# Sixteen experts in two forms: sorted by token count on the chip, the six smallest in plain float32 with gate and up side by side in TensorE's columns

## The chip, the cores and the metric

One core of one Trainium2 chip runs the whole kernel in one launch. The metric is the device time of one execution in microseconds (us), median of the runs shown. The two versions are compared on the same inputs.

## The reference, cut to what matters

Two layers run over 512 tokens of width 1024. Each has a part of mixers (attention, gated linear attention, mLSTM), then a mixture of experts, then a gated per-layer embedding. The mixture, on normalised tokens `t`:

```python
gi  = argmax(t @ w_group + b_group)               # one of 4 groups
el  = (t @ w_router + b_router)[group gi]          # its 4 experts
top_v, top_i = top_k(el, 2)
top_w = softmax(top_v) * softmax(group logits)[gi]
for e in range(16):
    a = silu(t @ w_gate[e]) * (t @ w_up[e])        # 1024 -> 512
    y = y + comb[:, e] * (a @ w_down[e])           # 512 -> 1024
```

Each token goes to two of the 16 experts, so an expert has 64 tokens on average. The reference's own routing of its inputs gives, with experts 0 and 1 left out and the other fourteen sorted, 73 72 72 71 71 70 65 62 and then 61 60 58 55 46 45 tokens in the first layer, and 106 98 91 87 65 65 61 56 and then 53 53 48 48 46 44 in the second.

## The kernel before, in words

All tensors are float32. Where precision matters a matmul is made of three: both factors are split into a high and a low part of type float32r (`split` and `hilo`: ScalarE copies the high part, VectorE subtracts it), and `mm3` (L328) multiplies high by high, high by low and low by high.

`moe` (L1294) does one layer's mixture. The token rows are stored to DRAM (`xd`, L1297). Routing: rank comparisons give each token's two experts, a cumulative count on TensorE gives its place in the expert's list, and `rows`, `places` and `to_rows` turn this into lists of row numbers, one column for each expert: `ix` (row to gather) and `iy` (row to scatter to). `parts` and `to_parts` bring two scales for each row the same way, `sw`: the combine weight and the token's inverse norm.

The experts run in the order 0 to 15. For expert `e`:

- `fetch(e)` (L1588) gathers up to `CAP` = 112 rows by an indirect DMA on GpSimd's queue; numbers past the count are out of bounds and move nothing. `scale` multiplies by the norm's gain.
- `x_T` and `x_split` transpose the rows (8 transposes of 128 columns) and split them.
- `gate_up(c, u)`: eight calls, four for gate and four for up. Each splits two of the eight 128-row blocks of the weight matrix and issues 6 matmuls of 512 columns: 48 for gate and up together.
- `silu`, `times`, `a_T` (4 transposes), `a_split`, and `down(k)` for four k: 24 matmuls of 512 columns.
- `store` (L1538) copies the result times its weight to `YE` and scatters the rows into `yd` in DRAM by an indirect DMA (L1548).

The loop (L1598) staggers this: round `e` does the gate and up of expert `e`, the transposes of expert `e`+1, the down matmuls of expert `e`-1 and the store of expert `e`-2.

Weights come by plain DMAs on SyncE's queue (`load`, L259): 1 MB each, two for gate, two for up, two for down, 6 MB for an expert. Sixteen buffers of 1 MB take turns (`E8O`), so a load waits until the sixteenth load before it has been split. The first loads are issued while the mixers still run; the sixteenth goes to ScalarE's queue (`late`). After expert 15 the per-layer embedding follows: `ple_prep` and `ple_rows` multiply the embedding (`PR`), a branch (L1680) handles experts with over 112 tokens, and the rows of `yd` are loaded as `Y` (L1729) and added to `X` (L1755). Everything after that needs `X`.

A scheduler sets the order of instructions on each engine from the program's order and its own costs.

Of the kernel before, what the change touches and what calls it, by code (L numbers as in the profile page):

```python
# [14 lines left out]
I32 = mybir.dt.int32  # L15
# [12 lines left out]
CAP = 112  # L28
# [38 lines left out]
def tile_encoder(ctx: ExitStack, tc: tile.TileContext, A, out):  # L67
# [132 lines left out]
    v.tensor_copy(tok, ti)  # L200
    cs_.__exit__(None, None, None)
# [46 lines left out]
    def load(src, eng=nc.sync):  # L248
# [9 lines left out]
        late = NQ < st["n"] <= E8  # L258
        i = (nc.scalar if late else eng).dma_start(wv, src)  # L259
        if late:  # L260
            order(st["ex"], i)
        elif NP < st["n"] <= E8 + 1:
            order(st["xd"], i)
# [302 lines left out]
    def mixers(l, T_):  # L566
# [652 lines left out]
        def router_weights():  # L1219
# [8 lines left out]
            g.tensor_tensor(wr3, wr3, bc(gc.unsqueeze(2), [128, 8, 20]), OP.mult)  # L1228
            wrs = small("wrs", 320, F32R, bufs=1)
# [64 lines left out]
    def moe(l, X, rsx, lg3):  # L1294
# [75 lines left out]
        def parts():  # L1370

            V = t2("V2")[:, 0:384].bitcast(BF16).rearrange("p (j i c e) -> p j i c e", j=N8, i=3, c=2)
            ra = small("ra", 2 * N8, bufs=1)
            rb_ = small("rb_", 2 * N8, BF16, bufs=1)
            g.tensor_copy(ra[:, 0:N8], w12)
            g.tensor_copy(ra[:, N8:2 * N8].rearrange("p (k t) -> p k t", k=2), bc(rsx.unsqueeze(1), [128, 2, NT]))
            for i in range(3):
                g.tensor_copy(rb_, ra)
                st["parts"] = g.tensor_tensor(V[:, :, i, :, :], bc(oh3.unsqueeze(2), [128, N8, 2, 16]),
                                bc(rb_.rearrange("p (c j) -> p j c", c=2).unsqueeze(3), [128, N8, 2, 16]), OP.mult)  # L1380
                if i < 2:
                    g.tensor_tensor(ra, ra, rb_, OP.subtract)
            return V

        def to_rows(dst, V, O, c):

            ps = mm()[:, 0:16]
            for j in range(N8):
                pe.matmul(ps, O[:, j, :], V[:, j, 0, :], start=(j == 0), stop=False)
                st["pe"] = pe.matmul(ps, O[:, j, :], V[:, j, 1 + c, :], start=False, stop=(j == N8 - 1))  # L1390
            return v.tensor_scalar(dst, ps, 1024.0 * (1 + c), None, OP.add)

        def to_parts(dst, V, O):

            ps = mm()[:, 0:32]
            for j in range(N8):
                for i in range(3):
                    pe.matmul(ps, O[:, j, :], V[:, j, i].rearrange("p c e -> p (c e)"), start=(j == i == 0), stop=(j == N8 - 1 and i == 2))
            act(dst, ps, AF.Copy)
# [5 lines left out]
        ix, iy = small("ix", 16, I32, bufs=1), small("iy", 16, I32, bufs=1)  # L1405
        st["gate"] = to_rows(ix, V1, OH, 0)
# [5 lines left out]
        to_rows(iy, V1, OH, 1)  # L1412
        st["wm"] = warm(W2, st["pe"])
        cmax = small("cmax", 1, bufs=1)
        after(v.tensor_reduce(cmax, pos[:, 64:80], AX.X, OP.max))
        cmi = small("cmi", 17, I32, bufs=1)
        v.tensor_copy(cmi[:, 16:17], cmax)
        after(v.tensor_copy(cmi[:, 0:16], pos[:, 64:80]))
# [24 lines left out]
        sw = small("sw", 32, bufs=1)  # L1443
# [26 lines left out]
        class Expert:  # L1470


            def __init__(self, n, w_, xe, iyc, swc, rsc, m=CAP):
                self.n, self.w, self.xe, self.iyc, self.swc, self.rsc, self.m = n, w_, xe, iyc[0:m], swc[0:m], rsc[0:m], m
# [17 lines left out]
            def gate_up(self, c, u):  # L1492

                if u == 0:
# [15 lines left out]
            def times(self):  # L1510
                v.scalar_tensor_tensor(self.a, self.pu[0:self.m], self.rsc, self.a, OP.mult, OP.mult)
# [15 lines left out]
            def down(self, k):  # L1527

                if k == 0:
                    self.py = [zb(), zb()]  # L1530
# [3 lines left out]
                for half in range(2):  # L1534
                    hs = slice(half * 512, half * 512 + 512)
                    _, self.last = mm3(self.py[half][0:self.m], self.ah[:, k, :], self.al[:, k, :], hi[:, 0, hs], lo[:, 0, hs], k == 0, k == 3)

            def store(self, both=False):  # L1538
# [4 lines left out]
                act(ye[:, 0:512], self.py[0][0:self.m], AF.Copy, scale=self.swc)  # L1543
# [307 lines left out]
```

## Time and profile before

| what | value |
|---|---|
| median of 3 runs (lowest, highest) | 1462.6 us (1461.03, 1466.82) |
| profiled execution: its own time, its span | 1467.49 us, 1465.8 us |
| granted TensorE clock, mean | 0.978 |
| TensorE, VectorE, ScalarE, GpSimd busy | 95%, 82%, 67%, 23% |
| moved by DMA | 304.39 MB, 208 GB/s over the span |

The span runs from the first instruction to the last; the execution's own time is 1.7 us more. The two mixtures lie at about 350 to 669 us and 1075 to 1393 us. A matmul's duration in a row includes the time it takes to run through the array, which the next ones overlap, so the pace of matmuls is read from the distances of their starts.

### The profile page before, as it was taken

What the parts mean: (1) busy time and instruction counts of PE and PEld (TensorE: products, weight loads), DVE (VectorE), ACT (ScalarE), POOL (GpSimd) and SP (SyncE); (2) the same over time, 40 slices, a digit from 0 to 9 for tenths busy, and PEclk for the clock granted to TensorE, in tenths of its full rate; (3) what the DMA queues carried; (4) which work ended last, traced back from release to release, by engine and by line L of the source; (5) the groups of instructions that cost most, each with busy time, mean ns of one, the idle gap of its engine ahead of it and who ended that gap; (6) DMA issues with size and microseconds to landing.
All of it is one profiled execution on the core that took longest, in us unless ns stands there. A gap on an engine that the chain in (4) does not pass through costs nothing. (4 is left out here: it accounts for less than half of the span.)

```text
span 1465.8 us, 23792 instructions
## 1 busy us (share of the span) xinstructions
PE 1386.5 (95%) x8468; PEld 1139.5 (78%) x8468; DVE 1197.9 (82%) x2057; ACT 981.5 (67%) x1747; POOL 338.8 (23%) x356
## 2 busy tenths in 40 slices
PE   6998999998899999998989989999979999999997
PEld 5787878995677777777967878789957777777787
DVE  5779887567799999997667788866679999999875
ACT  5553675645688888886555546655458888888864
POOL 4223000211243333312012230002013434333000
PEclk9999999999899999999979999999989999999999
DMA  6321133648799999937133112326478999999271
GB/s 164 102 65 54 58 85 83 230 139 298 234 380 379 374 375 374 380 109 255 49 122 100 56 32 72 102 80 227 162 277 297 371 371 373 365 360 357 92 245 58
DMA packets 171235, 304.39 MB, mean 208 GB/s; under 512 B 30368, under 2 KB 69316, under 8 KB 171108
## 3 DMA queue, kind: packets, MB, share of 16 engines
q1 hardware_dynamic: 142656, 277.91, 54.7%
q0 software_dynamic: 9024, 18.99, 3.8%
q10 hardware_dynamic: 19428, 5.88, 1.7%
q8 instruction: 69, 1.13, 0.3%
q14 instruction: 58, 0.48, 0.1%
HBM read 285.90 MB, written 23.13 MB: 211 GB/s over the span
## 5 line engine op out<-in xcount | busy, mean ns | idle before, releaser
L293 DVE TENSOR_TENSOR lo<-we,hi 128x1024 fp32r<-128x1024 f32 x380 | 447.3, 1222 | 17.7 <-PE mm L330 5.8
L237 ACT ACTIVATE hi<-we 128x1024 fp32r<-128x1024 f32 x380 | 396.4, 1059 | 78.9 <-PE mm L331 46.1
L329 PE MATMUL mm<-hi,xhl 128*112 128x512 f32 x480 | 193.4, 403 | 0.3 <-POOL gqattn_k_norm_g L611 0.3
L331 PE MATMUL mm<-hi,xhl 128*112 128x512 f32 x480 | 191.3, 399 | 1.3 <-DVE xhl L336 1.3
L1548 POOL DMA_INDIRECT yd<-YE,iy x32 | 143.2, 4475 | 203.0 <-ACT YE L237 81.7
L330 PE MATMUL mm<-lo,xhl 128*112 128x512 f32 x480 | 190.0, 396 | 0.0
L482 PE MATMUL zb<-hi,Th 128*128 128x256 f32 x576 | 169.3, 295 | 0.0
L483 PE MATMUL zb<-lo,Th 128*128 128x256 f32 x576 | 163.1, 283 | 0.0
L484 PE MATMUL zb<-hi,Tl 128*128 128x256 f32 x576 | 162.3, 282 | 0.0
L482 PEld LDWEIGHTS zb<-hi,Th 128*128 128x128 f32 x576 | 109.0, 190 | 8.8 <-issue 8.0
L483 PEld LDWEIGHTS zb<-lo,Th 128*128 128x128 f32 x576 | 109.2, 190 | 2.9 <-issue 1.7
L484 PEld LDWEIGHTS zb<-hi,Tl 128*128 128x128 f32 x576 | 108.9, 189 | 1.5 <-issue 1.3
L331 PEld LDWEIGHTS mm<-hi,xhl 128*112 128x112 f32 x480 | 84.4, 176 | 29.3 <-DVE xhl L336 1.4
L330 PEld LDWEIGHTS mm<-lo,xhl 128*112 128x112 f32 x480 | 84.7, 176 | 26.5
L329 PEld LDWEIGHTS mm<-hi,xhl 128*112 128x112 f32 x480 | 84.7, 176 | 25.6 <-POOL gqattn_k_norm_g L611 0.5
L329 PE MATMUL zb<-hi,ah 128*112 128x512 f32 x256 | 103.4, 404 | 1.0 <-ACT ah L237 1.0
L331 PE MATMUL zb<-hi,al 128*112 128x512 f32 x256 | 101.4, 397 | 0.0
L330 PE MATMUL zb<-lo,ah 128*112 128x512 f32 x256 | 101.1, 395 | 0.0
L293 DVE TENSOR_TENSOR lo<-w,hi 128x1024 fp32r<-128x1024 f32 (+3 forms) x66 | 74.9, 1134 | 24.3 <-PE zb L483 18.0
L237 ACT ACTIVATE hi<-w 128x1024 fp32r<-128x1024 f32 (+3 forms) x66 | 63.0, 955 | 38.3 <-PE zb L484 35.8
L237 ACT ACTIVATE P<-mm,nm 128x512 f32<-128x512 f32 x64 | 44.0, 688 | 39.4 <-DVE nm L1012 39.0
L482 PE MATMUL zb<-hi,mh 128*128 128x256 f32 x224 | 65.0, 290 | 1.4 <-DVE X L1134 1.4
(426 smaller groups left out, 3278.3 us busy)
## 6 DMA issues: line engine op xcount, KB each, us to landing
we<-in_w_expert_up_dram SPq DMA_DIRECT2D x64, 1024.0 KB, 11.7
we<-in_w_expert_down_dram SPq DMA_DIRECT2D x64, 1024.0 KB, 12.8
we<-in_w_expert_gate_dram SPq DMA_DIRECT2D x60, 1024.0 KB, 12.0
w<-in_w_in_dram SPq DMA_DIRECT2D x44, 512.0 KB, 3.8
we<-in_w_ple_gate_dram SPq DMA_DIRECT2D x8, 1024.0 KB, 9.7
Y<-yd SPq DMA_DIRECT2D x16, 512.0 KB, 9.5
X<-xd SPq DMA_DIRECT2D x12, 512.0 KB, 4.0
w<-in_w_out_dram SPq DMA_DIRECT2D x10, 512.0 KB, 4.4
```

Of the source, the lines that this page charges most:

```text
L237: i = s.activation(out_, in_, func, **kw)
L293: i = (g if eng == "g" else v).tensor_tensor(l3, src, h3.bitcast(F32), OP.subtract)
L329: i = pe.matmul(ps, ah, bh, start=start, stop=False)
L330: pe.matmul(ps, ah, bl, start=False, stop=False)
L331: return i, pe.matmul(ps, al, bh, start=False, stop=stop)
L482: pe.matmul(pt[tb], ah[c][:, sl], hi, start=(k == 0 and (by_tb or tb % 2 == 0)), stop=False, skip_group_check=True)
L483: pe.matmul(pt[tb], ah[c][:, sl], lo, start=False, stop=False, skip_group_check=True)
L484: pe.matmul(pt[tb], al[c][:, sl], hi, start=False, stop=(k == nk - 1), skip_group_check=True)
L1548: st["sc"] = g.indirect_dma_start(out=yv[self.n], out_offset=bass.IndirectOffsetOnAxis(ap=self.iyc, axis=0), in_=ye, in_offset=None, bound ...
```

## The change

The experts get 16 slots. Slots 0 and 1 hold experts 0 and 1 always; the other fourteen are ranked by token count, largest first, by comparisons on VectorE (`c2`, `se`, `eq`). `by_slot` permutes the expert numbers (`pi`) and the lists of rows and scales (`ixs`, `iys`, `rps`) into slot order. SyncE reads each slot's expert number from `pi` into a register, and the loads of slots 2 to 15 take their address from it. Slots 0 to 9 run as before; slots 10 to 15 are of class `Small`: 64 rows at most, the factors unsplit in float32, gate's result in PSUM partitions 0 to 63 and up's in 64 to 127, so that gate's weights-by-rows matmul uses one half of the array's columns and up's the other; `down` does the same with its two halves of 512 output columns. The combine weight moves from `store` to the addition of `Y`, where it is a column for each token (`wr`). The branch now runs for a count above 112 in a big slot or above 64 in a small one. All loads go by SyncE's queue.

```diff
-CAP = 112
+CAP, CAPS, NBIG = 112, 64, 10
...
-        late = NQ < st["n"] <= E8
-        i = (nc.scalar if late else eng).dma_start(wv, src)
+        i = eng.dma_start(wv, src)
...
+        sq_ = t2("eq")
+        aux, eq = [sq_[:, c:c + 256].rearrange("p (s e) -> p s e", s=16) for c in (0, 256)]
+        cn = small("cn", 16, bufs=1)
+        after(v.tensor_copy(cn, pos[:, 64:80]))
+        c2, se = small("c2", 16, bufs=1), small("se", 16, bufs=1)
+        v.scalar_tensor_tensor(c2, cn, 16.0, tie, OP.mult, OP.add)
+        v.tensor_tensor(aux, bc(c2.unsqueeze(1), [128, 16, 16]), bc(c2.unsqueeze(2), [128, 16, 16]), OP.is_gt)
+        v.tensor_reduce(se, aux, AX.X, OP.add)
+        v.tensor_tensor(eq, bc(se.unsqueeze(1), [128, 16, 16]), bc(io16.unsqueeze(2), [128, 16, 16]), OP.is_equal)
+
+        def by_slot(dst, src):
+
+            v.tensor_tensor(aux, eq, bc(src.unsqueeze(1), [128, 16, 16]), OP.mult)
+            return v.tensor_reduce(dst, aux, AX.X, OP.add)
...
+        by_slot(pf, io16)
+        v.tensor_copy(pi, pf)
...
+        class Small(Expert):
...
+            def x_split(self, q):
+                if q == 0:
+                    self.x = r3(t8("xhl")[:, 0:512], 8)
+                    v.tensor_tensor(self.x, r3(self.ps, 8), bc(st["gc"].unsqueeze(2), [128, 8, 64]), OP.mult)
+
+            def gate_up(self, k):
+
+                if k == 0:
+                    self.pg = mm()
+                if k % 4 == 0:
+                    self.rw = [load(self.w(nm).rearrange("(k p) n -> p k n", p=128)[:, k:k + 4, :]) for nm in ("w_expert_gate", "w_expert_up")]
+                for c in range(2):
+                    pe.matmul(self.pg[64 * c:64 * c + 64], self.x[:, k, :], self.rw[c][:, k % 4, :], start=(k == 0), stop=(k == KD - 1))
...
+            def down(self, k):
...
+                for h in range(2):
+                    pe.matmul(self.py[h], self.aT[:, k, :], self.rd[k][:, 0, h * 512:h * 512 + 512], start=(k == 0), stop=(k == 3))
...
+            m, ic = (CAP if e < NBIG else CAPS), (ix if e < 2 else ixs)[:, e:e + 1]
+            if e < 2:
+                w_ = lambda nm: A[nm][l, e]
+            else:
+                pv = nc.values_load(pi[0:1, e:e + 1], engines=[mybir.EngineType.SP], min_val=0, max_val=15)
+                w_ = lambda nm: A[nm][l][bass.DynSlice(pv, 1)].rearrange("o k n -> (o k) n")
+            EX.append((Expert if e < NBIG else Small)(e, w_, gather(ic, e, m), iys[:, e:e + 1], rps[:, e:e + 1], m))
...
-        with tc.If(cnt > CAP):
+        with tc.If(cnt > 0):
...
-                    i = (g if (tb, h) in XA else v).tensor_tensor(X[tb][:, hs], X[tb][:, hs], Y[tb][:, k, hs], OP.add)
+                    i = v.scalar_tensor_tensor(X[tb][:, hs], Y[tb][:, k, hs], wr[:, c:c + 1], X[tb][:, hs], OP.mult, OP.add)
```

SyncE's queue, first layer, from the loads of the first experts to the first ones that need the sort. Before:

```order
L259 DMA we<-in_w_expert_down_dram 128x2x1024 x2
L259 DMA we<-in_w_expert_gate_dram 128x4x512 x2
L259 DMA we<-in_w_expert_up_dram 128x4x512 x2
L1297 DMA xd<-X 128x1024 x4
L259 DMA we<-in_w_expert_down_dram 128x2x1024 x2
L1679 TENSOR_LOAD cmi
```

And now (`pi` is the list of expert numbers; the `ISA` rows set registers):

```order
L265 DMA we<-in_w_expert_down_dram 128x2x1024 x3
L1302 DMA xd<-X 128x1024 x4
L265 DMA we<-in_w_expert_down_dram 128x2x1024
L1686 TENSOR_LOAD pi
L1686 ISA x2
...
L265 ISA
L265 DMA we<-in_w_expert_gate_dram 128x4x512
L265 ISA
L265 DMA we<-in_w_expert_gate_dram 128x4x512
```

The four loads of expert 2's gate and up stood ahead of the store of `xd`; those of slot 2 now stand behind it and behind the reading of `pi`.

VectorE, first layer, from the first list of rows to the scaling of the first gathered rows (`lo<-W` is a weight split, `XE` the gathered rows, `xhl` the split of the transposed rows). Before:

```order
L1391 TENSOR_SCALAR ix<-mm 128x16
...
L1442 TENSOR_TENSOR w_4593<-w_4593,ex 128x4
L293 TENSOR_TENSOR lo<-W_4461,hi 128x1024
L1466 TENSOR_TENSOR XE<-XE,gain 112x1024
L293 TENSOR_TENSOR lo<-W_4461,hi 128x1024
L1466 TENSOR_TENSOR XE<-XE,gain 112x1024
L336 TENSOR_TENSOR xhl<-tp,xhl 128x4x112 x2
```

And now:

```order
L1400 TENSOR_SCALAR ix<-mm 128x16
...
L1482 TENSOR_TENSOR w_4625<-w_4625,ex 128x4
L1508 TENSOR_TENSOR XE<-XE,gain 112x1024
L1438 TENSOR_REDUCE pf<-eq 128x16
L297 TENSOR_TENSOR lo<-W_4467,hi 128x1024
L1400 TENSOR_SCALAR iys<-pf 128x16
L340 TENSOR_TENSOR xhl<-tp,xhl 128x4x112 x2
L297 TENSOR_TENSOR lo<-W_4467,hi 128x1024
L1508 TENSOR_TENSOR XE<-XE,gain 112x1024
```

Between the first row and the row of `w` the sort adds 15 instructions, 8 of them of 256 elements. The first expert's `xhl` no longer stands behind the scaling of the second expert's rows.

TensorE at the end of the first layer's mixture as it is now (a row counts a float32 matmul once; `we` is a weight buffer, `aT` the transposed activations):

```order
L1614 MATMUL mm<-we,xhl 64x512 x16
L1640 MATMUL zb<-we,aT 64x512 x4
L1626 MATMUL tp<-ident,a 128x64 x4
L1640 MATMUL zb<-we,aT 64x512 x12
L1655 MATMUL tp<-ident,p 128x128 x8
L1775 TENSOR_LOAD cmi
```

These are the gate and up of slot 15, the down matmuls of slots 14 and 15 and the transposes of the embedding. The 48 and 24 matmuls of the last expert before have become 16 and 8.

## Rows read from the trace of the kernel before

**Rows 1.** Stretches: length, engines' busy time (instructions), clock, DMA share, GB/s
```profile
340.00:380.00 40.00, 28.64 (x179) 18.36 (x178) 27.89 (x69) 21.64 (x41) 9.48 (x15) 0.79 0.70 245
460.00:500.00 40.00, 40.00 (x188) 30.50 (x187) 38.89 (x39) 34.97 (x42) 16.99 (x7) 1.00 1.04 376
620.00:660.00 40.00, 39.48 (x184) 29.96 (x183) 36.82 (x36) 34.81 (x41) 7.09 (x3) 1.00 0.36 131
```

**Rows 2.** Transposes of gathered rows, eight an expert: their line, 440 to 640; timeline
```profile
L1481 PE MATMUL tp<-ident,XE x88: 257/259/260, 453.9 to 633.5; 112*128 112x112 f32 x88
...
632.81 0.93 PE L1481 MATMUL tp<-ident,XE 112*128 112x112 f32 x8
```

**Rows 3.** Weight loads by tile: all from 412.6, then the first, the last, `p`
```profile
L259 SPq DMA_DIRECT2D we<-in_w_expert_gate_dram x21: 367/368/368, 412.7 to 591.3; - x21
...
DMA to landing us min/median/max: 9.0/9.0/9.0
...
DMA to landing us min/median/max: 16.6/16.6/16.6
...
L1553 SPq DMA_DIRECT2D p<-in_p_dram x1: 368/368/368, 614.9 to 614.9; - x1
...
DMA to landing us min/median/max: 13.8/13.8/13.8
```

**Rows 4.** Second layer's last expert but one load, by tile
```profile
L259 SPq DMA_DIRECT2D we<-in_w_expert_down_dram x1: 994/994/994, 1336.0 to 1336.0; - x1
...
DMA to landing us min/median/max: 15.2/15.2/15.2
```

**Rows 5.** Timeline, ends of both mixtures: TensorE, the last scatter, the first load of `Y`
```profile
663.47 0.60 PE L1564 MATMUL tp<-ident,p 128*128 128x128 f32 x4
665.18 0.94 POOL L1548 DMA_INDIRECT yd<-YE,iy  x1 [6.60 <-ACTq L1680]
669.14 0.90 SPq L1729 DMA_DIRECT2D Y<-yd  x2
...
1387.00 0.60 PE L1564 MATMUL tp<-ident,p 128*128 128x128 f32 x4
1392.68 1.68 SPq L1729 DMA_DIRECT2D Y<-yd  x3
```

**Rows 6.** Scatters into `yd` by tile, issued at 622.65 and at 665.18: time to landing
```profile
DMA to landing us min/median/max: 9.7/9.7/9.7
...
DMA to landing us min/median/max: 3.8/3.8/3.8
```

**Rows 7.** Timeline of TensorE: float32 in column halves (L889) and whole (L873)
```profile
63.43 1.08 PE L889 MATMUL mm<-tT,la 128*64 128x256 f32 x8
64.44 0.39 PE L482 MATMUL zb<-hi,Th 128*128 128x256 f32 x1
...
70.48 1.02 PE L873 MATMUL mm<-la,tR 128*128 128x256 f32 x4
71.34 0.38 PE L878 MATMUL mm<-ident,qk 128*128 128x128 f32 x2
```

**Rows 8.** Timeline, routing and first expert: VectorE, SyncE, TensorE
```profile
357.60 0.42 DVE L1359 TENSOR_TENSOR V<-oh,tok 128x256 bf16<-128x256 f32 x1
363.03 0.21 DVE L1439 TENSOR_SCALAR w<-ex 128x4 f32<-128x4 f32 x1 [1.20 <-ACT ex L237]
363.76 1.23 DVE L293 TENSOR_TENSOR lo<-W,hi 128x1024 fp32r<-128x1024 f32 x1
367.83 1.23 DVE L1466 TENSOR_TENSOR XE<-XE,gain 112x1024 f32<-112x1024 f32 x1 [2.85 <-DMA XE<-xd,ix]
...
335.74 0.92 SPq L259 DMA_DIRECT2D we<-in_w_expert_gate_dram  x2
...
375.00 0.63 PE L329 MATMUL mm<-hi,xhl 128*112 128x512 f32 x1
375.42 0.63 PE L330 MATMUL mm<-lo,xhl 128*112 128x512 f32 x1
```

More of the change, by code (lines that the diff above doesn't have):

```diff
@@ L200, in tile_encoder @@
     v.tensor_copy(tok, ti)
+    io16 = const.tile([128, 16], F32, name="io16")
+    v.tensor_copy(io16, ii[:, 0:16])
+    tie = const.tile([128, 16], F32, name="tie")
+    v.tensor_scalar(tie, io16, -1.0, 15.0, OP.mult, OP.add)
+    for n in range(2):
+        v.memset(tie[:, n:n + 1], 65536.0 * (2 - n))
     cs_.__exit__(None, None, None)
@@ L1370, in parts @@
         def parts():
[L1372 to L1376, printed above, removed]
+            V = t2("V2")[:, 0:192].bitcast(BF16).rearrange("p (j i e) -> p j i e", j=N8, i=3)
+            ra = small("ra", NT, bufs=1)
+            rb_ = small("rb_", NT, BF16, bufs=1)
+            g.tensor_copy(ra, rsx)
             for i in range(3):
                 g.tensor_copy(rb_, ra)
-                st["parts"] = g.tensor_tensor(V[:, :, i, :, :], bc(oh3.unsqueeze(2), [128, N8, 2, 16]),
-                                bc(rb_.rearrange("p (c j) -> p j c", c=2).unsqueeze(3), [128, N8, 2, 16]), OP.mult)
+                for k in range(2):
+                    js = slice(k * NT, k * NT + NT)
+                    st["parts"] = g.tensor_tensor(V[:, js, i, :], oh3[:, js], bc(rb_.unsqueeze(2), [128, NT, 16]), OP.mult)
                 if i < 2:
@@ L1404, in moe @@
         OH = places()
-        ix, iy = small("ix", 16, I32, bufs=1), small("iy", 16, I32, bufs=1)
-        st["gate"] = to_rows(ix, V1, OH, 0)
+        ix, iy, ixs, iys = [small(nm, 16, I32, bufs=1) for nm in ("ix", "iy", "ixs", "iys")]
+        psx = to_rows(V1, OH, 0)
+        st["gate"] = number(ix, psx, 0)
         def after(i):
@@ L1535, in down @@
                     hs = slice(half * 512, half * 512 + 512)
[L1536 removed]
+                    mm3(self.py[half], self.ah[:, k, :], self.al[:, k, :], hi[:, 0, hs], lo[:, 0, hs], k == 0, k == 3)
             def store(self, both=False):
@@ L1691, in moe @@
                     ce = nc.values_load(cc[0:1, 0:1], min_val=0, max_val=T)
-                    with tc.If(ce > CAP):
+                    with tc.If(ce > 0):
                         ic, jc = [small(nm, 1, I32, bufs=1) for nm in ("ic", "jc")]
-                        wc, rc_ = [small(nm, 1, bufs=1) for nm in ("wc", "rc_")]
-                        for d_, s_, o_ in ((ic, ix, 0), (jc, iy, 0), (wc, sw, 0), (rc_, sw, 16)):
-                            v.tensor_copy(d_, s_[:, bass.DynSlice(e_ + o_, 1)])
+                        rc_ = small("rc_", 1, bufs=1)
+                        for d_, s_ in ((ic, ix), (jc, iy), (rc_, rp)):
+                            v.tensor_copy(d_, s_[:, bass.DynSlice(e_, 1)])
                         w_ = lambda nm: A[nm][l][bass.DynSlice(e_, 1)].rearrange("o k n -> (o k) n")
-                        ex = Expert(16, w_, gather(ic, 0, 128), jc, wc, rc_, 128)
+                        ex = Expert(16, w_, gather(ic, 0, 128), jc, rc_, 128)
                         scale(ex.xe, 128)
@@ L1702, in moe @@
                             ex.x_split(q)
-                        for c in range(2):
-                            for u in range(4):
-                                turn[0] = s0 + 6 + c
-                                ex.gate_up(c, u)
+                        for u in range(8):
+                            turn[0] = s0 + 6 + u // 4
+                            ex.gate_up(u)
                         ex.silu()
```

114 lines of the change are left out of this document (74 added, 40 removed).

## The prediction

> **What bounds the kernel now.** I read the stretches first, then the weight loads by tile, then the ends of the two mixtures. In the middle of a mixture TensorE is busy 40.00 us of 40, and the DMA engines are full as well, a share of 1.04 at 376 GB/s [rows 1]. Two limits lie close together, and the change moves only one of them, so each needs its own pace.
>
> TensorE's pace: the transposes of eleven experts begin between 453.9 and 633.5. Less the 0.7 us between the first and the last of one expert's eight, that is 178.9 us for ten experts, **17.9 us an expert** [rows 2]. The DMA engines' pace: the gate load issued at 412.7 landed after 9.0 us, the one at 591.3 after 16.6. They are twenty gate loads apart, two an expert, so ten experts. The landings lie at 421.7 and 607.9, **18.6 us an expert** [rows 3]. The engines are slower than TensorE uses the weights up, and the delay grows by 0.7 us an expert. That is why I count them as full and don't expect them to go faster.
>
> Yet the weights don't set the end. The embedding `p`, issued behind the last weights, landed at 614.9 + 13.8 = 628.7. Its 0.5 MB take 1.4 us at 376 GB/s, so the last weights were there at 627.3 [rows 1, 3]. TensorE finished the last down matmul at 663.5 [rows 5]. For 36 us it worked off full buffers, with the DMA share down at 0.36 [rows 1]. In the second layer the last load but one landed at 1336.0 + 15.2 = 1351.2, the last 2.8 us later (1 MB), at 1354.0 [rows 4]; TensorE finished at 1387.0, 33 us later [rows 5]. From TensorE's end to the first load of `Y`, which all that follows needs, it is 5.7 us in both layers [rows 5].
>
> **The small experts on TensorE.** A float32 matmul leaves two records in the trace. Whole-array ones of 256 columns start 0.215 us apart (four from 70.48, the next matmul at 71.34). In column halves eight such records take 1.01 us (63.43 to 64.44) [rows 7]. Taking turns they would need 8 x 0.215 = 1.72; in pairs 4 x 0.215 = 0.86. So the halves run together, and 0.15 is left over, which I count once for each change between halves and whole. For 512 columns a step is 0.43. Gate and up take 8 blocks x 2 steps, down 4 x 2: 24 x 0.43 = 10.3 us. Twelve transposes take at most 0.12 each (0.93 / 8, [rows 2]), 1.4; they have 64 columns in place of 112, so half of that at the low end. Four changes of form add 0.6. Together 11 to 12.3, and I take **12**. If the 0.15 were not fixed but a share of the work (1.01 / 0.86), the 10.3 would be 12.1 and the expert 14.1; this is the high end.
>
> "Mode switching requires drain", says the Trainium skill (TensorEngine Tiling, Key Properties). It speaks against a form that alternates halves with whole-array transposes, and the 0.15 agrees with a small drain. By the rule alone, without a figure, the sum could not be made.
>
> Six experts save 6 x (17.9 - 12) = 35.4 us of TensorE a layer. The weights limit what of this is seen: the small expert needs 12 us and its weights 18.6. After the last load only the last two blocks of down are left, 4 steps, 1.7 us. First layer: TensorE's limit is 663.5 - 35.4 = 628.1, the weights' limit 627.3 + 1.7 = 629.0. Second layer: 1387.0 - 35.4 = 1351.6 and 1354.0 + 1.7 = 1355.7. The weights win in both, and TensorE ends 34.5 and 31.3 us earlier.
>
> **What follows the last matmul.** `YE`, the branch and the scatter remain, 5.7 us. But the scatter used to meet idle DMA engines and landed in 3.8 us; under load one took 9.7 [rows 6]. Now it comes right behind the weights, among `p`, the embedding's weights and `X`, 3.5 MB or 9.3 us of transfers. So 0 to 6 us are given back a layer; being issued some 4 us into that queue, it gets the middle, 3. Gains: 31.5 and 28.3, **59.8 us**. TensorE's embedding matmuls, which run beside the loads of `Y`, move with it; the embedding's weights land about 3 us after the experts', still ahead of `Y`.
>
> **The sort.** It puts 15 instructions on VectorE between the first list of rows and the first scaling: 8 of 256 elements at 0.42 and 7 small ones at about 0.18, 4.6 us. There VectorE sat idle 1.20 and 2.85 us, and the weight split of 1.23 goes behind [rows 8]. This covers 5.3, and the scaling waits for the gathered rows in any case: cost 0. Without that cover it would be 4.6 a layer. The first expert's low parts no longer wait behind the second expert's gather, which may give up to 2 us back; I take none, because the weight split has moved behind. Gather lists of slot 2 and scatter lists are needed later.
>
> **The loads that now wait for the sort.** Expert 2's gate and up were issued at 335.7 and just after, before the store of `xd` [rows 8]. Now four loads, and the one that went by ScalarE's queue, wait for `pi`, at about 365. Four take 4 x 2.8 = 11.2 us. The DMA engines were 30% idle between 340 and 380, 12 us [rows 1], and the slot starts only two experts after the first, near 410. So they fit: cost 0, but tightly, and 11.2 us a layer if they don't, as every later load queues behind them. Behind SyncE's wait stand only loads of later slots. Its register settings are small beside the 3.0 us between loads (17.9 / 6); an issue takes 0.46.
>
> **Edits at nothing.** Splits that go, on ScalarE and VectorE, were paced by TensorE. The combine weight is one more operand in an addition that is made anyway. The small experts' gather moves no fewer bytes: numbers out of bounds never moved. The second layer's router gain is now loaded late, behind slot 15's `x_split`, ahead of the last silu on ScalarE; it has one expert's 18.6 us to land.
>
> **The sum.** 1467.5 - 59.8 = 1407.7 for the profiled execution, which was 4.9 above the median of the runs: **1403**. Differences under 0.5% can't be told from none here.
>
> **Rivals.**
> - *The early loads are not caught up* (or a small expert takes 14.1). For it: 12 us of idle for 11.2 us of loads, and the idle lies partly before `pi` is there. Against: the buffers are full by 380 either way, and the engines have slack until about 400. Price 11.2 a layer: 1425. For 14.1: 6 x 2.1 = 13 less, the first layer then ends near 641, about the same price.
> - *The clock stays low, slower.* Small experts leave TensorE idle a third of the time. Between 340 and 380, busy 28.64 of 40, the granted clock was 0.79 on average, and the first expert's matmuls ran at the lower of the two levels, 1.2 GHz, 0.42 us apart [rows 1, 8]. At 1.2 GHz a step is 0.86, the expert 24 x 0.86 + 2 = 22.6. From 17.9 on it is a loss: 6 x 4.7 = 28 a layer, 1519. Against: at 22.6 TensorE would be behind the weights and would not pause, and without pauses it was granted 1.00 [rows 1]. So it decides only if the clock stays low under steady work. Pauses in matmul work bring the half clock, says the Trainium skill (TensorE: Matmul & The Clock Gate, HAM oscillation); the trace agrees in its 0.79. By that rule alone, held through all small experts, the time would be that of this rival.
> - *The halves take turns at 512 columns, slower.* 48 x 0.43 + 2 = 22.6, the same 1519. Against: rows 7, unless twice the columns change it.
> - *It doesn't do what it says:* were a small slot over 64 tokens, the branch would run. By the reference's routing the largest small slot has 61 and 53, no big one over 106. Then there is no gain or a large loss.
>
> **Chances.** Forecast 0.75, with 1388 to 1418 as its own range: 3 us a layer either way from the scatter, 2 a layer from the start, some from the weights' pace. The first rival 0.15, at 1418 to 1432. The two slower ones 0.05 and 0.03, no gain 0.02. The range goes from 1386 to 1428, which leaves out the slow cases and the worst of the first rival. Faster by over 0.5% holds the forecast and the first rival, with a little off for what I have not seen: 0.90; within 0.5%: 0.02; slower: 0.08.
>
> **What would show it.** Right: in the last third of each mixture TensorE is busy about two thirds, with DMA still near 375 GB/s until the last weights; small records in pairs of starts, steps of 0.43; the first load of `Y` near 638 in the first layer, the second layer's about 60 earlier than now; VectorE's first scaling still waits for the gather. Wrong: a DMA gap before slot 2's loads with weights landing 11 us later (first rival); steps of 0.86 or single starts (the slower ones); instructions of the branch's body.

## The result, and the profile after

| | before | after |
|---|---|---|
| median of 4 runs each, one chip | 1461.82 us (1460.81 to 1466.82) | 1417.28 us (1415.28 to 1418.67) |
| profiled execution: own time, span | 1467.49, 1465.8 us | 1418.6, 1416.9 us |
| TensorE, VectorE, ScalarE busy | 95%, 82%, 67% | 93%, 72%, 58% |

The ratio is 0.9688, its 95% interval 0.9661 to 0.9715: faster by 44.5 us, where I forecast 59.8. In the two profiled executions the first load of `Y` comes 24.8 us earlier in the first layer (669.14 to 644.34) and 49.0 in the second (1392.68 to 1343.68); the span ends 48.9 earlier. So the whole gain lies in the two mixtures, 24.8 and 24.2, against 31.5 and 28.3 forecast, and what stands between them gives and takes next to nothing.

The stretches of the changed kernel (columns as in [rows 1]):

```profile
340.00:380.00 40.00, 33.35 (x218) 22.13 (x217) 35.28 (x95) 26.27 (x47) 12.72 (x20) 0.87 0.63 206
460.00:500.00 40.00, 40.00 (x190) 30.84 (x189) 39.00 (x39) 34.57 (x41) 15.43 (x7) 1.00 1.02 370
580.00:620.00 40.00, 30.26 (x130) 9.41 (x127) 3.62 (x6) 3.73 (x6) 1.85 (x2) 1.00 1.05 379
620.00:660.00 40.00, 30.88 (x144) 18.80 (x142) 17.95 (x30) 18.82 (x33) 9.82 (x15) 0.91 0.89 319
```

In the third row, among the small experts, TensorE is busy 30 of 40 us at full clock while the DMA engines are full: the weights set the pace. Against [rows 1] the share between 620 and 660 is 0.89 instead of 0.36, so the weights now last until the end. What TensorE waited for between 580 and 636 (us in total, times, the longest) says the same:

```profile
PE mm L1614 <- DMA we<-in_w_expert_up_dram: 11.1, 6, 2.2
PE zb L1640 <- DMA we<-in_w_expert_down_dram: 1.3, 2, 1.0
PE mm L1614 <- DMA we<-in_w_expert_gate_dram: 0.4, 2, 0.2
```

Where weights are at hand, a small expert shows its own time. Timeline of TensorE, L1614 gate and up, L1600 and L1626 transposes, L1640 down:

```profile
559.58 4.51 PE L1614 MATMUL mm<-we,xhl 128*64 128x512 f32 x20
564.02 0.71 PE L1600 MATMUL tp<-ident,XE 64*128 64x64 f32 x8
564.67 3.65 PE L1640 MATMUL zb<-we,aT 128*64 128x512 f32 x16
568.15 2.75 PE L1614 MATMUL mm<-we,xhl 128*64 128x512 f32 x12
570.83 0.46 PE L1626 MATMUL tp<-ident,a 64*128 64x64 f32 x4
571.22 4.51 PE L1614 MATMUL mm<-we,xhl 128*64 128x512 f32 x20
```

From 559.58 to 571.22 it is 11.64 us; the twenty records begin 0.206 apart on average, two to a matmul, so 0.41 a step.

The end of the first mixture (timelines of TensorE, GpSimd and SyncE), answering to [rows 5]:

```profile
634.04 1.94 PE L1640 MATMUL zb<-we,aT 128*64 128x512 f32 x8 [0.97 <-DMA we<-in_w_expert_down_dram]
635.91 1.09 PE L1655 MATMUL tp<-ident,p 128*128 128x128 f32 x8
...
637.67 0.90 POOL L1591 DMA_INDIRECT yd<-YE,iys  x1 [4.35 <-DVE YE L1588]
...
644.34 1.97 SPq L1824 DMA_DIRECT2D Y<-yd  x4
...
1343.68 1.96 SPq L1824 DMA_DIRECT2D Y<-yd  x4
```

The last weights are there at 634.0; I had 627.3. The scatter landed after 6.5 us. And the start (timelines of VectorE, SyncE, TensorE), answering to [rows 8]:

```profile
364.91 0.19 DVE L1443 CAST pi<-pf 128x16 int32<-128x16 f32 x1
367.18 1.28 DVE L1508 TENSOR_TENSOR XE<-XE,gain 112x1024 f32<-112x1024 f32 x1 [0.53 <-DMA XE<-xd,ix]
...
367.31 1.01 SPq L265 DMA_DIRECT2D we<-in_w_expert_gate_dram  x2
368.51 1.25 SPq L265 DMA_DIRECT2D we<-in_w_expert_up_dram  x2
...
371.41 0.40 PE L333 MATMUL mm<-hi,xhl 128*112 128x512 f32 x1
371.64 0.39 PE L334 MATMUL mm<-lo,xhl 128*112 128x512 f32 x1
```

Slot 2's loads go out at 367.31, 31.6 us later than before, as forecast. What I had not forecast: the first expert's matmuls follow each other every 0.23 us at 371.4, where they went every 0.42 at 375.0.

Two theories for the missing gain, which the first experiments are to tell apart. **Start** (my first rival): the loads behind the sort are not caught up, and the weights end later by them. **Rate**: 50 us behind the first store of the rows (`xd`) both kernels had moved about the same bytes in the first layer; after that, up to 580, the DMA engines only gave 358 to 370 GB/s, where they gave 374 to 379 before.

### The profile page after: what moved, and what is told of

The parts are those of the page before. It is cut to its first block, busy times and chain, and to the rows that moved or that the text cites. A ratio compares the mean times of both kernels' runs of the same rounds, so it can differ in the third digit from the quotient of the medians.

```text
span 1416.9 us, 23046 instructions
## 1 busy us (share of the span) xinstructions
PE 1318.4 (93%) x8180; PEld 1024.5 (72%) x8180; DVE 1018.7 (72%) x1931; ACT 816.7 (58%) x1565; POOL 290.7 (21%) x362
## 5 line engine op out<-in xcount | busy, mean ns | idle before, releaser
L297 DVE TENSOR_TENSOR lo<-we,hi 128x1024 fp32r<-128x1024 f32 x236 | 276.7, 1219 | 5.9 <-ACT hi L244 2.0
L244 ACT ACTIVATE hi<-we 128x1024 fp32r<-128x1024 f32 x236 | 246.0, 1059 | 47.6 <-PE mm L335 24.6
L1591 POOL DMA_INDIRECT yd<-YE,iys x32 | 87.8, 2745 | 181.3 <-ACT YE L244 173.1
L1614 PE MATMUL mm<-we,xhl 128*64 128x512 f32 x384 | 95.7, 599 | 22.6 <-DMA we<-in_w_expert_up_dram 21.3
L333 PE MATMUL mm<-hi,xhl 128*112 128x512 f32 x288 | 114.2, 398 | 0.6 <-issue 0.6
L334 PE MATMUL mm<-lo,xhl 128*112 128x512 f32 x288 | 113.6, 394 | 0.0
L335 PE MATMUL mm<-hi,xhl 128*112 128x512 f32 x288 | 113.2, 393 | 0.0
L1614 PEld LDWEIGHTS mm<-we,xhl 128*64 128x64 f32 x384 | 27.6, 136 | 82.2 <-issue 43.2
L244 ACT ACTIVATE a<-mm,rps 112x512 f32<-112x512 f32 (+1 forms) x32 | 21.9, 686 | 96.1 <-PE mm L1614 78.3
L244 ACT ACTIVATE YE<-zb 112x512 f32<-112x512 f32 (+1 forms) x62 | 34.7, 589 | 50.9 <-PE zb L1640 37.1
L333 PE MATMUL zb<-hi,ah 128*112 128x512 f32 x160 | 64.0, 402 | 0.0
```

The lines of the kernel that those rows point to most:

```text
L244: i = s.activation(out_, in_, func, **kw)
L297: i = (g if eng == "g" else v).tensor_tensor(l3, src, h3.bitcast(F32), OP.subtract)
L333: i = pe.matmul(ps, ah, bh, start=start, stop=False)
L334: pe.matmul(ps, ah, bl, start=False, stop=False)
L335: return i, pe.matmul(ps, al, bh, start=False, stop=stop)
L1591: st["sc"] = g.indirect_dma_start(out=yv[self.n], out_offset=bass.IndirectOffsetOnAxis(ap=self.iyc, axis=0), in_=ye, in_offset=None, bound ...
```

## The experiments

Each ratio is to the kernel before, run on the same chip, with its 95% interval. Not all experiments ran on one chip; the kernel before had medians from 1461.8 to 1465.2 us on them, so a difference of two experiments' times is good to some 3 us.

**Slot 2 fixed.** The table that ties slots to experts gets a third entry, and slot 2 takes its weights and rows without the sort.

```diff
-    for n in range(2):
-        v.memset(tie[:, n:n + 1], 65536.0 * (2 - n))
+    for n in range(3):
+        v.memset(tie[:, n:n + 1], 65536.0 * (3 - n))
...
-            m, ic = (CAP if e < NBIG else CAPS), (ix if e < 2 else ixs)[:, e:e + 1]
-            if e < 2:
+            m, ic = (CAP if e < NBIG else CAPS), (ix if e < 3 else ixs)[:, e:e + 1]
+            if e < 3:
```

> Slot 2 is always expert 2 again, beside slots 0 and 1, so its four loads wait for no sort; the six smallest are picked from the other thirteen. Computes the reference. In the changed kernel the last weights were there at about 634.0 in the first layer where I had forecast 627.3. Theory Start (the four loads that wait for the sort are not caught up): the weights end some 6 us earlier a layer, 1417 - 12 = about 1405. Theory Rate (both kernels had moved about the same bytes 50 us behind the first store of the rows, and the changed one then moved 358 to 369 GB/s up to 580 where the one before moved 374 to 380): 1415 to 1417, at most 1 us a layer better, and the rate between 420 and 580 stays near 365.

Measured: 1403.81 us, 0.9595 (0.9557 to 0.9632). Timelines of SyncE and TensorE:

```profile
335.38 0.92 SPq L265 DMA_DIRECT2D we<-in_w_expert_gate_dram  x2
336.47 2.53 SPq L265 DMA_DIRECT2D we<-in_w_expert_up_dram  x2
...
625.46 1.94 PE L1640 MATMUL zb<-we,aT 128*64 128x512 f32 x8 [0.81 <-SPq L1776]
...
636.17 0.88 SPq L1824 DMA_DIRECT2D Y<-yd  x2
```

Counted from the first store of the rows, the last down matmuls begin 7.0 us earlier than in the changed kernel in the first layer and 7.8 in the second, where the profile puts their wait down to the weights. Start holds: 13.5 us are the four loads. Rate falls as the cause of these: from 500 to 580 this run had 353 and 366 GB/s, no more than the changed kernel's 364 and 358, and still gained.

The bytes show how both go together. From 40 us ahead of the first store to 50 us behind it, first layer, the kernel before, the changed one and this run (columns as in [rows 1]):

```profile
308.16:398.16 90.00, 77.92 (x520) 62.65 (x520) 65.00 (x141) 47.93 (x92) 11.88 (x18) 0.91 0.68 227
309.31:399.31 90.00, 82.64 (x553) 65.99 (x553) 74.39 (x166) 53.42 (x96) 17.38 (x22) 0.94 0.66 225
307.77:397.77 90.00, 81.42 (x549) 65.88 (x549) 73.88 (x166) 52.43 (x96) 13.27 (x22) 0.94 0.73 250
```

That is 20.4, 20.3 and 22.5 MB. Against the kernel before, which had stopped loading with its buffers full, the changed one is level; against this run it lacks 2.2 MB, 6 us at 376 GB/s. The lower rate costs something as well: the changed kernel, level at 50 us, has its last weights of this layer 5.6 us behind the forecast's 627.3, counted from the first store, and this run, 2.1 MB or 5.6 us ahead at 50 us, only 1.5 us ahead of it.

**The sort alone.** No slot is small.

```diff
-CAP, CAPS, NBIG = 112, 64, 10
+CAP, CAPS, NBIG = 112, 64, 16
```

> The sort stays, but all sixteen slots are big ones (three-part products, 112 rows): the sort alone. Computes the reference. My prediction (sort costs nothing, early loads are caught up, TensorE sets the end): within 3 us of the kernel before, 1459 to 1465. Theory Start: the four late loads would delay the weights by 11 us a layer but the weights have 36 us of slack here, so no change either: 1459 to 1465, and the start of the first expert's matmuls, 3 us earlier than before, may show as 3 us a layer, 1456. Rival (the sort itself lies on the path, 4.6 us a layer): 1471. Its DMA rate between 420 and 580: near 365 if sorted or computed addresses are slower to load from, near 376 if not.

Measured: 1449.36 us, 0.9896 (0.9859 to 0.9934), 366 to 370 GB/s between 420 and 580. None of the theories had this much: the sort costs nothing, and the code around it gives 15 us. Two things differ from the kernel before. The transposes of eleven experts, taken as in [rows 2], now give 17.66 us an expert in place of 17.89; fourteen of those are 3.2 us a layer. The rest comes at the start. In the kernel before, TensorE paused before the first transposes, and its granted clock then stood at 0.5 for 10.2 us. Its timeline:

```profile
369.21 0.96 PE L1481 MATMUL tp<-ident,XE 112*128 112x112 f32 x8 [2.62 <-DVE XE L1466]
```

In the run of the sort alone the pause is short, and the clock does not fall again. TensorE's timeline:

```profile
368.69 0.96 PE L1523 MATMUL tp<-ident,XE 112*128 112x112 f32 x8 [0.72 <-DVE XE L1508]
```

**A quarter of up.** The small slots load one block of four of `w_expert_up`.

```diff
-                    self.rw = [load(self.w(nm).rearrange("(k p) n -> p k n", p=128)[:, k:k + 4, :]) for nm in ("w_expert_gate", "w_expert_up")]
+                    self.rw = [load(self.w(nm).rearrange("(k p) n -> p k n", p=128)[:, k:k + q, :]) for nm, q in (("w_expert_gate", 4), ("w_expert_up", 1))]
...
-                    pe.matmul(self.pg[64 * c:64 * c + 64], self.x[:, k, :], self.rw[c][:, k % 4, :], start=(k == 0), stop=(k == KD - 1))
+                    pe.matmul(self.pg[64 * c:64 * c + 64], self.x[:, k, :], self.rw[c][:, 0 if c else k % 4, :], start=(k == 0), stop=(k == KD - 1))
```

> The six small slots load one of every four blocks of w_expert_up and use it for all four (the same matmuls, so the up product is another one); 9.4 MB or some 25 us of DMA time a layer less. If the weights set the end in the changed kernel, as predicted: TensorE's own limit shows, last down matmul at 628 in the first layer (663.5 - 35.4), where the changed kernel has 635.8; gain 7 us in the first layer, and 5 to 8 in the second, 1402 to 1406. If TensorE or a chain of waits in the small slots set it: no change, 1415 to 1419. If the small slot's own time is 14 rather than 12 us: 640, no change.

Measured: 1384.57 us, 0.946 (0.9424 to 0.9496): 33 us under the changed kernel, more than twice what I expected. That the weights set the end is shown, and TensorE's own limit lies lower than I had it: the last down matmul ends 273.8 and 268.9 us behind the first store of the rows, where my 628.1 and 1351.6 are 279.9 and 276.1. Between 570 and 636 no wait for weights is left. Another one shows there, 3.2 us for ScalarE's copies into `YE`. Waits of TensorE (us in total, times, the longest):

```profile
PE zb L1640 <- ACT YE L244: 3.2, 2, 2.6
```

**Weights in natural order.** The table that gives SyncE a slot's expert is filled with 0 to 15 before the routing.

```diff
+        pi = small("pi", 16, I32, bufs=1)
+        v.tensor_copy(pi, io16)
...
-        v.tensor_copy(pi, pf)
```

> The table that gives SyncE the expert of a slot holds 0 to 15 in natural order and is there before the routing is done; rows, counts and lists of rows are still sorted, so slots 2 to 15 multiply their rows with another expert's weights. Loads are still addressed by a register, but none waits for the sort, and the addresses run through memory in order. Theory Start: as in the run with slot 2 fixed, about 1405. Theory Rate with the order of the addresses as its cause: the rate between 420 and 580 is back at 374 to 380, 1408 to 1412. Theory Rate with another cause (addressing by register, the rows gathered, or chance of the execution): 1414 to 1417, rate near 365.

Measured: 1405.3 us, 0.96 (0.9561 to 0.9639). It has the time of the run with slot 2 fixed, and 361 and 351 GB/s between 500 and 580. The order of the addresses is not what lowers the rate there. Start again, by another way of not waiting.

**All big, natural order.** As the run of the sort alone, with all sixteen entries tied, so that the sort returns the natural order, and no load waits for it.

```diff
-    for n in range(2):
-        v.memset(tie[:, n:n + 1], 65536.0 * (2 - n))
+    for n in range(16):
+        v.memset(tie[:, n:n + 1], 65536.0 * (16 - n))
```

> All sixteen slots are big and in natural order with weights addressed without a register; the instructions of the sort stay on VectorE (they put every expert at its own number), but no load waits for them. Computes the reference. The sorted run with all slots big had 1449.4, 16 us under the kernel before. In its trace the first gather landed after 4.7 us where the kernel before had 6.2, TensorE's granted clock did not fall a second time at the first expert's matmuls (before: 10.2 us at 0.5 in the first layer, 3.4 in the second), and an expert took 17.66 us in place of 17.89. Theory Empty queue (the gain at the start comes because slot 2's loads no longer stand before the gather): the gather is late again and the clock falls, 1455 to 1460, with only the pace kept (14 x 0.23 = 3.2 us a layer). Theory Order (it comes from the order on VectorE and GpSimd, in which the first expert's low parts stand before the second expert's gather): 1447 to 1452.

Measured: 1455.95 us, 0.9938 (0.9917 to 0.9958), inside Empty queue: 6.6 us of the 15 go with loads that no longer stand before the first gather. It landed after 7.1 us here, 6.2 in the kernel before, 4.6 in the run of the sort alone. SyncE's timeline has three loads in front of the gather, where the kernel before had two and the run of the sort alone one. The number alone doesn't set the time: with two in front it also landed after 4.6 (embedding behind the scatter) and 4.9 (longer bridge). TensorE's row is the last:

```profile
354.80 1.32 SPq L265 DMA_DIRECT2D we<-in_w_expert_down_dram  x2
356.17 0.53 SPq L265 DMA_DIRECT2D we<-in_w_expert_gate_dram  x1
...
371.39 1.73 PE L1523 MATMUL tp<-ident,XE 112*128 112x112 f32 x8 [3.48 <-DVE XE L1508]
```

The pause is back, and so is the half clock, for 6.8 us in the first layer. The pace of 17.66 us stayed, which accounts for 6.4 of the 7.8 us that are left.

**Longer bridge of ones, kernel before.**

```diff
-W1, W2 = 0, 22
+W1, W2 = 0, 31
```

> The kernel before with 31 in place of 22 matmuls of ones between the routing and the first expert's transposes, nothing else; they last to about 368.7 where they ended at 366.2, so that TensorE pauses 0.5 us before the first transposes in place of 3.0. Computes the reference. Theory Clock (the start's gain in the changed kernel comes from the granted clock, which in the kernel before fell to 0.5 for 10.2 us in the first layer and 3.4 in the second at the first expert's matmuls): no second fall, 5.1 + 1.7 us less, 1455 to 1458. Theory Order (it is the wait of the first expert's low parts for the second gather): the fall may go, but the matmuls still wait, 1461 to 1464.

Measured: 1467.72 us, 1.0018 (1.0001 to 1.0034): no gain. The pause before the transposes is gone, also because the first gather landed after 4.9 us in this execution, but it comes back two gate matmuls later, at the low parts, and the clock falls there, for 6.8 us. TensorE's timeline:

```profile
368.09 0.93 PE L1481 MATMUL tp<-ident,XE 112*128 112x112 f32 x8
...
375.21 0.77 PE L331 MATMUL mm<-hi,xhl 128*112 128x512 f32 x1 [3.41 <-DVE xhl L336]
```

**Low parts first, kernel before.** The second scaling is ordered behind the first expert's low parts.

```diff
-                scale(EX[e + 1].xe, after=st["lo"] if e else None)
+                scale(EX[e + 1].xe, after=st["lo"] if e else cur.xi[1])
```

> The kernel before with one order on VectorE changed: the second expert's first scaling, which waits for the second gather, stands behind the low parts of the first expert's rows, as it does in the changed kernel. Computes the reference. In the trace of the kernel before the low parts began at 373.76, 1.2 us behind the landing of the second gather; nothing else kept them. Theory Order (this wait is what the start cost): the low parts begin by 371.3, and TensorE's granted clock falls for less than 10.2 us or not at all: 2 to 6 us a layer, 1453 to 1461. Theory Empty queue (only loads that don't stand before the first gather help): within 2 us of the kernel before, 1463 to 1467.

Measured: 1464.01 us, 0.9999 (0.998 to 1.0017). The low parts did begin earlier, 370.50 for 373.76, and it gave nothing. Order alone falls: the first gather still comes late, TensorE then waits for `V`, a routing table from GpSimd, in place of the low parts (0.49 and 2.01 us; 0.78 before), and between 360 and 380 the granted clock is 0.68 on average (0.67 before, 0.88 in the run of the sort alone). Timelines of VectorE and TensorE:

```profile
370.50 1.14 DVE L336 TENSOR_TENSOR xhl<-tp,xhl 128x448 fp32r<-128x448 f32 x2
...
373.61 0.61 PE L1398 MATMUL mm<-V,OH 128*128 128x32 bf16 x17 [2.01 <-POOL V L1379]
```

The stretch, columns as in [rows 1]:

```profile
360.00:380.00 20.00, 14.68 (x70) 8.36 (x69) 11.22 (x24) 5.83 (x9) 11.30 (x14) 0.68 0.42 130
```

In the kernel before, TensorE meets pauses in a row: for the first gather, for `V`, for the low parts behind the second gather. Each edit took away one, another stayed or grew, and neither paid. The changed kernel has none of them. Both edits together were not tried on the kernel before.

**Embedding behind the scatter.** With slot 2 fixed, `p`, the projection and the gate's first quarter go to GpSimd's queue. Only `p` is ordered behind the last scatter.

```diff
-            nc.sync.dma_start(pr, A["p"][l].rearrange("(t p) f -> p t f", p=128))
-            return pr, load(A["w_ple_proj"][l].rearrange("(k p) n -> p k n", p=128))
+            order(st["sc"], nc.gpsimd.dma_start(pr, A["p"][l].rearrange("(t p) f -> p t f", p=128)))
+            return pr, load(A["w_ple_proj"][l].rearrange("(k p) n -> p k n", p=128), nc.gpsimd)
...
-        pw = ple_load()
+        pt = turn[0]
         EX[14].store()
...
         prev.store(True)
+        t_, turn[0] = turn[0], pt
+        pw = ple_load()
+        turn[0] = t_
...
-        wg.append(wcols(A["w_ple_gate"][l], 0, 256))
+        wg.append(wcols(A["w_ple_gate"][l], 0, 256, nc.gpsimd))
```

> The kernel with slot 2 fixed; the embedding rows p, the embedding's projection and the first quarter of its gate are issued by GpSimd behind the last scatter, so that they don't stand before it (2.5 MB). Computes the reference. The prediction's term (a scatter under load costs 3 us a layer: it landed after 6.5 us in the changed kernel, 3.8 before): the first loads of Y some 2.7 us earlier a layer, 1397 to 1400 if nothing else waits. Rival (TensorE waits for the embedding's projection, which lands 10 us later, and the transfers of Y queue behind): given back, 1403 to 1410.

Measured: 1433.53 us, 0.9788 (0.976 to 0.9816), worse than the rival said. The expectation had the projection and the gate's quarter behind the last scatter too; the trace has them far ahead of it. The last scatter landed after 3.2 us, so the price of 3 us for loads in front of it is right, but `p` was missing. Timelines of GpSimd and TensorE:

```profile
593.77 0.80 POOL L265 DMA_DIRECT2D we<-in_w_ple_proj_dram  x1 [9.44 <-PE zb L1640]
...
608.06 0.96 POOL L265 DMA_DIRECT2D we<-in_w_ple_gate_dram  x1 [12.05 <-PE mm L1614]
...
636.91 0.90 POOL L1591 DMA_INDIRECT yd<-YE,iys  x1 [3.23 <-DVE YE L1588]
637.81 0.82 POOL L1644 DMA_DIRECT2D p<-in_p_dram  x1
...
642.38 1.94 PE L1655 MATMUL tp<-ident,p 128*128 128x128 f32 x8 [7.16 <-DMA p<-in_p_dram]
649.38 0.77 PE L333 MATMUL mm<-ph,pT 128*128 128x512 f32 x1 [5.06 <-PEq L1779]
```

The projection and the gate's quarter, 2 MB, go out among the last experts' weights, and the last down matmuls begin 5.4 us later than with slot 2 fixed, counted from the first store. Then comes the wait for `p`. The embedding's matmuls begin 14.2 us later by that count (649.4) and hold up all that follows. What the edit would have cost with all three loads behind the scatter was not tried.

**Long packets.** With slot 2 fixed, a partition holds neighbouring rows of the weights, for gate, up and down; the transposes take the columns to match, and the small slots load their gain in the same order.

```diff
-[...].rearrange("(k p) n -> p k n", p=128)
+[...].rearrange("(p k) n -> p k n", p=128)
...
-self.xe[:, kk * 128:(kk + 1) * 128]
+self.xe.rearrange("m (p k) -> m k p", k=8)[:, kk, :]
```

> The kernel with slot 2 fixed, and each partition holds neighbouring rows of the expert weights (row = partition x 8 + block in place of block x 128 + partition), so that a packet carries 8 KB in place of 2 KB (gate, up) or 4 KB (down); the transposes take every eighth or fourth column to match, and the small slots' gain is loaded in that order. Computes the reference. In the trace a packet of 2 KB took 92 ns in the mixture (22.3 bytes a ns), one of 4 KB 167 to 181, one of 8 KB elsewhere 324 (25.3). If the engines' time is set by packets: some 9 in 100 off the weights' 240 us, then TensorE sets the end; by the run with a quarter of up, its last down matmul lies 5.7 and 7.4 us earlier than with slot 2 fixed, so 1389 to 1393. If memory gives no more than 376 GB/s in any form: 1401 to 1406. If strided transposes are slower on TensorE, each small expert has 12 of them: over 1406.

Measured: 1393.12 us, 0.9519 (0.9493 to 0.9546): 10.7 us under the run with slot 2 fixed. The same bytes go in 86,368 packets where the changed kernel needs 143,712. Queues of this run (packets, MB, share of 16 engines' span):

```profile
q1 hardware_dynamic: 86368, 280.00, 56.1%
```

It delivered 369 to 384 GB/s between 420 and 580 (353 to 380 with slot 2 fixed), and TensorE waits for no expert weights any more after 570. It pays for that with strided transposes, 1.09 us for the eight of a small expert in place of 0.71, and 12.25 us for the expert in place of 11.64. TensorE's timeline:

```profile
567.53 1.09 PE L1602 MATMUL tp<-ident,XE 64*128 64x64 f32 x8
568.56 3.65 PE L1642 MATMUL zb<-we,aT 128*64 128x512 f32 x16
572.04 2.74 PE L1616 MATMUL mm<-we,xhl 128*64 128x512 f32 x12
574.72 0.69 PE L1628 MATMUL tp<-ident,a 64*128 64x64 f32 x4
575.34 4.51 PE L1616 MATMUL mm<-we,xhl 128*64 128x512 f32 x20
579.78 1.09 PE L1602 MATMUL tp<-ident,XE 64*128 64x64 f32 x8
```

The Trainium skill (Perfetto Trace Analysis, DMA Optimizations) advises larger transfers, 4 or 8 KB in place of 2, where DMA sets the time; this run agrees, with 10.7 us. The Trainium skill also says (SBUF — State Buffer, Door 1: The DMA port swizzle) that reads which leave their 16-byte line at each element are slower; here every eighth float is read, 32 bytes apart, and 1.09 against 0.71 agrees.

**Seven small slots**, three runs with long packets: slot 2 fixed to expert 2, slot 2 sorted, slot 2 fixed to expert 5.

```diff
-CAP, CAPS, NBIG = 112, 64, 10
+CAP, CAPS, NBIG = 112, 64, 9
```

> As the run with long packets, with seven small slots in place of six (the largest has 62 and 61 rows by the reference's routing). Computes the reference. If long packets make TensorE the one that sets the end: another 17.7 - 11.6 = 6 us a layer, 12 below that run, 1378 to 1382. If the weights still set the end: the same time as that run, within 3 us.

Measured: 1832.18 us, 1.251 (1.2475 to 1.2546). My expectation had the wrong list of rows: expert 2, one of the small ones with 55 rows, now sits in slot 2, so the seventh small slot got 65 rows in the first layer, one too many, and the branch ran. It shows in the count of the weight splits (groups by line: busy us, mean ns, idle before):

```profile
L297 DVE TENSOR_TENSOR lo<-we,hi 128x1024 fp32r<-128x1024 f32 x260 | 306.2, 1222 | 58.7 <-ACT hi L244 54.7 <-PE mm L334 0.2
```

Six small slots have 236 of them, and a seventh takes away 12 a layer, so 212 would be due; 48 more are four experts' worth, one in each of the branch's four passes. One row too many costs over 400 us.

> The changed kernel (slots 0 and 1 fixed, so slot 2's loads wait for the sort) with long packets and seven small slots; by the reference's routing slots 9 to 15 then hold 62 and 56 rows at most. Computes the reference. With long packets TensorE ran to the end of the mixture without a pause, a small expert took 12.25 us and a big one 17.9. If TensorE sets the end: one more small slot gives 2 x 5.65, from 1393.1 to 1381.8, and the late loads cost nothing or give 3 us a layer back at the start (the first gather meets idle engines): 1375 to 1382. If the weights set it again, the late loads cost 7 us a layer: 1389 to 1396.

> As the run before it, but slot 2 is always expert 5, whose loads wait for no sort; slots 9 to 15 still hold 62 and 56 rows at most. Computes the reference. If TensorE sets the end with long packets: 1381 to 1385, as late loads cost nothing, and up to 6 us slower than the run before it, since the first gather stands behind these loads. If the weights set the end: 1378 to 1383 and some 14 us faster than the run before it.

Measured: sorted 1395.1 us, 0.9523 (0.9502 to 0.9545); slot 2 fixed 1386.63, 0.9467 (0.9446 to 0.9489). With the late loads the weights set the end again. Waits of TensorE between 580 and 624 in the sorted run:

```profile
PE mm L1616 <- DMA we<-in_w_expert_up_dram: 4.2, 3, 2.1
PE mm L1616 <- DMA we<-in_w_expert_gate_dram: 0.2, 1, 0.2
PE zb L1642 <- DMA we<-in_w_expert_down_dram: 0.2, 1, 0.2
```

The other run has no wait there at all, and is 8.5 us faster. So with long packets, too, the four late loads are not free. The run with slot 2 fixed to expert 5 is the fastest of those that use every expert's own weights in full, 31 us under the changed kernel, though it gained 6.5 us on the run with long packets where 11 were due and lies 1.6 above what I expected.

## Why the prediction was right, and where its sum was off

The sign, the bound and the mechanism of the small experts were right; 1417.3 lies in the range and 14 us above the predicted time. It lies inside the forecast's own range (1388 to 1418) by 0.7 us only, and what put it there is the mechanism of the first rival.

- **The weights limit what is seen of the small experts: right.** TensorE waits 11.1 us for up weights in the last stretch, and less to load gave 33 us.
- **The loads that now wait for the sort ("they fit: cost 0, but tightly"): the step that failed.** They cost 7.0 and 7.8 us a layer at the last down matmuls, 13.5 us in the medians. I set 11.2 us of transfers against 12 us of idle between 340 and 380, read off the kernel before. There 8.2 of the 12 lie behind 365, but only one weight load goes out there between 355 and 377, as the buffers are full: it was not time in which the queue worked off what it had. In the changed kernel the queue runs empty before `pi` is there (DMA share 0.01 from 345 to 350, 0.07 from 360 to 365) and is full from 370 to the end (1.04 from 370 to 400), so nothing later catches the loads up. My argument against the rival, full buffers by 380 and slack until about 400, did not hold. The first rival was the right mechanism; its 11.2 a layer was an upper end.
- **The weights' limit from the kernel before (627.3 and 1354.0): near for loads in time.** With slot 2 fixed TensorE stopped waiting 1.5 and 4.1 us earlier than that, counted from the first store. In the first layer two terms that I did not have work against each other: some 2 MB more by 400 us than in the kernel before, which I put down to the earlier start of the first expert, and the lower rate. That this run took 1403.8, the predicted 1403, is in part luck.
- **A small expert takes 12 us: 11.64.** (The low end of my sum adds up to 11.6, not to 11.) Steps of 0.41 for 0.43; the halves run in pairs. The four transposes of `a`, which begin 0.08 apart, and the change behind them take 0.39 (570.83 to 571.22), so 0.15 for the change again.
- **TensorE's limit (628.1 and 1351.6): too high by 6.1 and 7.2 us,** by the run with a quarter of up. The small experts are 0.36 shorter and the big ones 0.23, some 4.5 us together; the rest I put down to the start. It is hidden here by the weights and did not change the time.
- **The start ("up to 2 us back, I take none"): mis-sized.** With all slots big it was 15 us for two layers together with the pace, 6.6 of it with late loads that clear the way for the first gather. The wait has two faces: it delays the weights by 7 us a layer and lets TensorE begin earlier, and while the weights set the end only the first one counts.
- **The sort itself, cost 0 on VectorE: right.** The first scaling waited 0.53 us for the gather and not for the sort, and the run of the sort alone lost nothing.
- **A scatter under load, 3 us a layer: right.** 6.5 us in the changed kernel, 3.2 where neither `p` nor the embedding's weights stood right before it.
- **Edits at nothing:** no loss from them shows, but ScalarE's late `YE` cost TensorE 3.2 us as soon as the weights were out of the way.
- **The clock stays low, the halves take turns, no gain: none came.** The clock was granted at 1.00 through the small experts although TensorE paused a quarter of the time.
- **The marks:** the first load of `Y` at 644.34 where I said near 638, the second layer's 49 earlier where I said about 60.

The forecast was summed against an execution that lies 5.7 us above the median of these runs; the changed one's was 1.3 above. By the traces alone the gain is 10.9 us short of the forecast, by the medians 15.3.

What stays open: why the big experts' pace fell from 17.89 to 17.66 us in every kernel with the change, which was not tried apart; why seven small slots with long packets gained 6.5 us and not 11; and why the DMA engines give 351 to 369 GB/s from 500 to 580 in the kernels with 2 KB packets and small experts, where those with big ones alone have 367 to 376. The order of the addresses is excluded.

## What to carry to other kernels

When a change makes loads wait for data computed on the chip, idle DMA time counts only from the moment that the data is there. Idle time read off the old kernel can be that of full buffers, and goes when the engine behind them starts earlier; where a full queue follows, a late load comes back at the end. A small part of the order can be kept fixed, here one slot, so that its loads fill the time of the sort. Once transfers set the time, look at the packet size before cutting more work on TensorE.

## What was not expected of the hardware

- In the mixture, between 420 and 600, a packet of 2 KB took 92 ns on average (22.3 bytes a ns; kernel before), one of 8 KB 344 ns (23.8; long packets).
- Transposes of every eighth column of 64 rows took 1.09 us for eight, neighbouring columns 0.71.
- A pause of 2.6 us before eight transposes was followed by 10.2 us at half clock, one of 0.7 us by none; with that pause closed alone, the fall came at the next one (3.4 us; 6.8 us at half clock).
- The first gather of one expert's rows landed after 4.6 us with one weight load of 1 MB issued in the 9 us before it, after 4.6 to 6.2 with two, after 7.1 with three.
